# The second branch's gate columns moved to the front of an encoder layer, as two groups of 2x2 block quads

## The chip, the cores and the metric

The kernel runs on one core of one Trainium2 chip. The metric is device time in microseconds; the kernel before has a median of 1356.09 us over three runs (1355.71 to 1360.79). The names in the profile: PE is TensorE (matmuls; PEld its weight loads), DVE VectorE, ACT ScalarE, POOL GpSimd, and SP the engine that issues most transfers.

## The reference

One layer of an encoder over 256 tokens of width 2048, all in fp32. What matters here is the token-mixing half:

```python
h = rms_norm(x, g_mix)
proj = h @ w_in          # columns: c_q 512, c_kv 512, k_r 64, q_d, k_d, v_d 1024 each, gate 2 x 2048
c_q, c_kv, k_r, q_d, k_d, v_d, gate = jnp.split(proj, cuts, axis=-1)
...
y_a = o_a.reshape(B, S, MLA_HEADS * V_DIM) @ w_o_mla     # o_a: latent attention
y_b = o_b.reshape(B, S, dh) @ w_o_dil                    # o_b: dilated attention
g = jax.nn.sigmoid(gate + b_gate).reshape(B, S, 2, D_MODEL)
x = x + (g[:, :, 0] * y_a + g[:, :, 1] * y_b) @ w_o
gt, up = jnp.split(rms_norm(x, g_ffn) @ w_gate_up, 2, axis=-1)
return x + (jax.nn.silu(gt) * up) @ w_down
```

The gates depend on x and w_in alone, so they may be computed at any point before y_a and y_b are merged. The first branch's gates are gate columns 0 to 2047, the second's 2048 to 4095.

## The kernel before

**Products.** Every fp32 operand is split into a high part (a cast by ACT) and a low part (the rest, a subtraction by DVE), and each product is three matmuls: high by high, high by low, low by high (`mm3`, lines 428 to 431). The split itself is `split_pair` (lines 221 to 223), used for weights, which stream once through the chip, and for activations. x is transposed on PE in pairs of 128-column blocks k (`job_x`); `split_evac` (lines 205 to 219) takes a transposed pair out of PSUM, scaled by `g_mix`, as high part xTh (ACT, L214) and low part xTl (DVE, L219).

**Groups.** The work is a list of groups, each some columns of one weight matrix by all of its rows k. A group's weights come in chunks of 512 KB: SP loads a chunk into one of three buffers `x` (pool `xp`), ACT and DVE split it into one of six buffers of pool `wp`, and PE multiplies. `loads` and `splits` run a fixed number of chunks ahead of the products (`AHEAD`). In a group of w_in a chunk is two k, split as a 128x1024 cast and a 128x1024 subtraction. The list was: cq, ckv, group b0 of the dilated q, k, v, then four times (uq, ukv, b), b5, b6, the first branch's four gate groups `g0`, then for each j an output group of the latent attention, a gate group of the second branch, and an output group of the dilated attention (one behind), then four groups of w_o, and the FFN.

**Quads.** The FFN's w_gate_up groups are wider: gate and up columns together, 1024, and one step, a quad, is a 2x2 arrangement of blocks (two k, two column halves), multiplied into eight PSUM banks that are held for the whole stage. A plain quad has 8 block products, 24 matmuls. Quads 2, 4 and 6 (`FAST`) are multiplied with 7 block products, 21 matmuls, from sums of blocks: on the weights' side `split_fast` (lines 843 to 855) makes three additions on DVE and two further splits (rh/rl and r) before the wh/wl split; on the activations' side `job_h` (lines 615 to 635) copies the transposed blocks out as hs, and makes sums of them and splits them into hsh and hsl. `evac_fast` and `evac_pair` combine the banks at the end of the fast products and of the group.

**Order.** Up to the last two groups ahead of the FFN the program stands in written order (`in_order`, a manual schedule); after that a scheduler orders each engine's instructions by priority. Small jobs (transpositions, statistics of x, pieces of the attentions) are queued in `jobs` and `limited`, and one advances after each step; `needs` finishes a job at once when a product depends on it. Gate values went: banks, one `scalar_tensor_tensor` per token half (scale by 1/rms, add bias, L571), sigmoid on ACT (`evac_ya` for the first branch at its use, `evac_g1` at once for the second), and stayed in SBUF tiles until `evac_ya` and `evac_yb`. Each bias row is loaded by SP, broadcast over 128 partitions, 8 steps ahead.

Of the kernel before, what the change touches and what calls it, by code (L numbers as in the profile page):

```python
# [97 lines left out]
def layer_kernel(ctx: ExitStack, tc: tile.TileContext, a: dict, out: bass.AP):  # L98
# [142 lines left out]
    def transpose_in(act, k0, nk, src, gname=None):  # L241
# [315 lines left out]


# [15 lines left out]
    def evac_g0(j):  # L574
        def evac(ps, step):
            g0[j] = gate_evac(ps, j, f"g0_{j}")
        return evac

    def evac_ya(j):
# [3 lines left out]
        return evac  # L583
# [31 lines left out]
    def job_h(i):  # L615

        ps = half_side(f"tr_h{i}").rearrange("p (k s) -> p k s", s=S)
        for k in range(2):
            f = 2 * i + k
            for t in range(NT):  # L620
                nc.tensor.transpose(ps[:, k, t * P:(t + 1) * P], x1[f // 4][:, t, (f % 4) * P:(f % 4 + 1) * P], ident)
        g = [gain("g_ffn", 2 * i + k) for k in range(2)]
        if i not in EITHER:
            hP[i] = t4([P, 2, 2, S], f"hP{i}", F32R)
            split_evac(*((hP[i][:, 0, k], hP[i][:, 1, k], ps[:, k], g[k]) for k in range(2)))
        else:
            v, l, h = (t4([P, 8, P], f"{n}{i}", d) for n, d in (("hs", F32), ("hsl", F32R), ("hsh", F32R)))
            nc.scalar.activation(v[:, 0:8:7], ps[:, 0].rearrange("p (t s) -> p t s", t=NT), AF.Copy, scale=g[0])
            nc.scalar.activation(v[:, 1:3], ps[:, 1].rearrange("p (t s) -> p t s", t=NT), AF.Copy, scale=g[1])
            nc.vector.tensor_sub(v[:, 3], v[:, 7], v[:, 2])  # L630
            nc.vector.tensor_sub(v[:, 4], v[:, 7], v[:, 0])
            nc.vector.tensor_sub(v[:, 5], v[:, 0], v[:, 3])
            nc.vector.tensor_sub(v[:, 6], v[:, 1], v[:, 5])
            split_pair(h, l, v)
            hq[i] = (h, l)
        return
        yield
# [22 lines left out]
    def evac_fast(q):  # L660

        bank, z, u = held["q"], t4([P, NT, 512], f"z{q.group.c0}"), t4([P, NT, 512], f"u{q.group.c0}")
        add, sub = nc.vector.tensor_add, nc.vector.tensor_sub
        with tc.high_priority(offset=PRIO):
            nc.scalar.copy(u[:, 0], bank[1])
            sub(z[:, 0], bank[6], u[:, 0])
            add(u[:, 1], bank[7], z[:, 0])
            add(z[:, 1], bank[5], u[:, 1])
            add(z[:, 0], bank[5], z[:, 0])
        q.group.zu = z, u  # L670

    def evac_pair(half, i, last):

        def evac(zu, step):
            q = held["q"]
            z, u = zu
            add, sub = nc.vector.tensor_add, nc.vector.tensor_sub
            with tc.high_priority(offset=PRIO):
                add(z[:, 1], q[0], z[:, 1])
                add(z[:, 0], q[3], z[:, 0])  # L680
                add(u[:, 0], q[2], u[:, 0])
                sub(u[:, 1], q[4], u[:, 1])
# [44 lines left out]
    g_in(0, 512, evac_lat("cq"), sizes=[1, 1])  # L727
# [8 lines left out]
    for j in range(4):  # L736
        g_in(OFF_GATE + 512 * j, 512, evac_g0(j))
# [335 lines left out]
```

## Time and profile before

| | |
|---|---|
| median of three runs | 1356.09 us (1355.71 to 1360.79) |
| profiled execution | 1359.88 us, span 1358.1 us |
| mean granted clock of TensorE | 0.998 |
| matmuls on PE | 6243 |
| HBM read, written | 253.97 MB, 2.10 MB |

The page says how busy each engine was; the table of waits says, for each line of an engine, what its instructions waited for, how long in total, how often, and the longest. A row of a timeline gives the start in us, the duration, the engine, the line, the operation, the output and inputs by the program's names, the shapes, and in brackets the idle time before it and its releaser. A row of groups gives busy us in total, mean ns of one, and the idle time before the group's instructions with what ended it.

### The profile page before, as it was taken

Reading aid. Unit: us, or ns where it says so; the run is one execution under the profiler, and the core shown is the slowest. Engines: PE = TensorE matmul, PEld = TensorE weight load, DVE = VectorE, ACT = ScalarE, POOL = GpSimd, SP = SyncE. Lnnn points to the kernel's source line nnn. Section 1 sums busy time; section 2 is a strip of 40 time slices with the busy share of each in tenths; the row PEclk is TensorE's granted clock in tenths of the full one; section 3 lists DMA queues with packets and bytes.
Section 4 is the critical chain, followed back from the end, with each engine's and each line's share of the span. In section 5 each row is a group of like instructions: output and inputs, shape, how many; then the busy total and the mean of one; then the engine's idle time right before and its main releaser. Section 6 shows DMA issues by size and latency. Waiting matters only on the chain.

```text
span 1358.1 us, 16258 instructions
## 1 busy us (share of the span) xinstructions
PE 1338.5 (99%) x6243; PEld 1125.7 (83%) x6243; DVE 945.2 (70%) x916; ACT 653.0 (48%) x724; POOL 33.7 (2%) x41
## 2 busy tenths in 40 slices
PE   7999999999999999999999999999999999999998
PEld 5899999988888888888787888888878888888786
DVE  5567677677645555666789746886788579857973
ACT  6555655454444444455455433554445345434541
POOL 1010112000000000000000000000000000000000
PEclk9999999999999999999999999999999999999999
DMA  7555555656556665676545655556457555654662
GB/s 235 189 175 153 162 167 170 185 161 176 170 189 205 213 187 201 209 226 205 201 166 193 224 190 174 212 197 205 156 186 238 196 186 174 227 188 163 211 214 93
DMA packets 138733, 257.14 MB, mean 189 GB/s; under 512 B 9720, under 2 KB 29216, under 8 KB 138656
## 3 DMA queue, kind: packets, MB, share of 16 engines
q1 hardware_dynamic: 138288, 255.96, 58.1%
q8 instruction: 49, 0.80, 0.2%
q14 instruction: 28, 0.23, 0.1%
q10 hardware_dynamic: 144, 0.13, 0.0%
q0 software_dynamic: 224, 0.01, 0.0%
HBM read 253.97 MB, written 2.10 MB: 189 GB/s over the span
## 4 chain that ended last, share of the span: by engine, by line
PE 86%; DVE 5%; DMA 4%; issue 2%; ACT 2%; SPq 1%; DVEq 0%; ACTq 0%
PE g L431 14%; PE g L429 14%; PE g L430 14%; PE sC L429 5%; PE sC L430 5%; PE sC L431 5%; PE mA L429 3%; PE mA L431 3%; PE mA L430 3%; DMA x<-in_w_gate_up_dram 3%; PE sD L430 3%; PE sD L429 3%; PE sD L431 3%; PE mB L431 2%; PE mB L430 2%
## 5 line engine op out<-in xcount | busy, mean ns | idle before, releaser
L222 ACT CAST wh<-x 128x1024 fp32r<-128x1024 f32 (+3 forms) x349 | 465.0, 1352 | 427.9 <-DVE x L854 94.8
L223 DVE TENSOR_TENSOR wl<-x,wh 128x2048 fp32r<-128x2048 f32 x132 | 300.8, 2289 | 136.7 <-ACT wh L222 135.3
L223 DVE TENSOR_TENSOR wh<-x,wh 128x1024 fp32r<-128x1024 f32 (+2 forms) x217 | 250.7, 1172 | 110.2 <-ACT wh L222 108.7
L429 PE MATMUL g<-wh,xTh 128*128 128x512 f32 (+1 forms) x544 | 210.5, 387 | 2.1 <-ACT xTh L214 2.1
L431 PE MATMUL g<-wh,xTl 128*128 128x512 f32 (+1 forms) x544 | 207.9, 382 | 0.5 <-DVE xTl L219 0.5
L430 PE MATMUL g<-wh,xTh 128*128 128x512 f32 (+1 forms) x544 | 207.9, 382 | 0.0
L429 PEld LDWEIGHTS g<-wh,xTh 128*128 128x128 f32 x544 | 102.8, 189 | 17.5 <-ACT xTh L214 2.4
L431 PEld LDWEIGHTS g<-wh,xTl 128*128 128x128 f32 x544 | 102.9, 189 | 17.3 <-DVE xTl L219 1.0
L430 PEld LDWEIGHTS g<-wh,xTh 128*128 128x128 f32 x544 | 102.8, 189 | 15.4 <-DVE wh L223 0.3
L429 PE MATMUL sC<-wh,hP 128*128 128x512 f32 x220 | 86.1, 391 | 4.1 <-ACT z L685 2.3
L429 PE MATMUL sD<-wh,hP 128*128 128x512 f32 x220 | 85.7, 389 | 0.0
L431 PE MATMUL sD<-wh,hP 128*128 128x512 f32 x220 | 85.7, 389 | 0.0
L431 PE MATMUL sC<-wh,hP 128*128 128x512 f32 x220 | 85.6, 389 | 0.0
L430 PE MATMUL sC<-wl,hP 128*128 128x512 f32 x220 | 85.6, 389 | 0.0
L430 PE MATMUL sD<-wl,hP 128*128 128x512 f32 x220 | 85.6, 389 | 0.0
L222 ACT CAST rh<-x 128x1024 fp32r<-128x1024 f32 x33 | 34.7, 1051 | 44.6 <-DMA x<-in_w_gate_up_dram 44.6
L429 PEld LDWEIGHTS sC<-wh,hP 128*128 128x128 f32 x220 | 41.3, 188 | 14.9 <-issue 6.5
L429 PE MATMUL g<-wh,mTh 128*128 128x512 f32 x128 | 50.5, 394 | 0.0
L431 PE MATMUL g<-wh,mTl 128*128 128x512 f32 x128 | 49.9, 390 | 0.0
L430 PE MATMUL g<-wh,mTh 128*128 128x512 f32 x128 | 49.8, 389 | 0.0
L430 PEld LDWEIGHTS sD<-wl,hP 128*128 128x128 f32 x220 | 41.3, 188 | 8.7
L429 PEld LDWEIGHTS sD<-wh,hP 128*128 128x128 f32 x220 | 41.3, 188 | 8.7
(674 smaller groups left out, 2383.0 us busy)
## 6 DMA issues: line engine op xcount, KB each, us to landing
x<-in_w_gate_up_dram SPq DMA_DIRECT2D x143, 512.0 KB, 5.0
x<-in_w_down_dram SPq DMA_DIRECT2D x88, 512.0 KB, 5.1
x<-in_w_in_dram SPq DMA_DIRECT2D x79, 512.0 KB, 3.7
x<-in_w_in_dram SPq DMA_DIRECT2D x56, 448.0 KB, 3.5
x<-in_w_gate_up_dram SPq DMA_DIRECT2D x66, 256.0 KB, 3.0
x<-in_w_o_dram SPq DMA_DIRECT2D x32, 512.0 KB, 4.5
x<-in_w_o_mla_dram SPq DMA_DIRECT2D x16, 512.0 KB, 4.9
x<-in_w_o_dil_dram SPq DMA_DIRECT2D x16, 512.0 KB, 4.7
```

The lines of the kernel that those rows point to most:

```text
L222: nc.scalar.copy(h, x)
L223: nc.vector.tensor_sub(l, x, f32(h))
L429: nc.tensor.matmul(ps, ah, bh, start=first, stop=False)
L430: nc.tensor.matmul(ps, ah, bl, start=False, stop=False)
L431: nc.tensor.matmul(ps, al, bh, start=False, stop=last)
```

## The change

The first group is now the first branch's gate group 0 (with the small first chunks that cq had), then follow the second branch's gates as two quad groups of 1024 columns (gate columns 0 and 1, then 2 and 3, of 512 each), with the first branch's gate group 1 between them; then cq, ckv and the rest in their old order, with gate groups 2 and 3 of the first branch where all four were. In the quad groups quads 2, 4 and 6 are fast (`FAST_X`); for these, unsplit copies of x's transposed blocks are made when x is transposed (`copy_blocks`), and sums and splits of them a little later (`sums_of`, which the FFN now uses too, with 7 blocks split instead of 8). The finished second-branch gates (after sigmoid) and the unsigmoided values of the first branch's groups 0 and 1 are written to DRAM by GpSimd, 6 writes of 512 KB, and read back by SP 8 steps before their use. Bias rows are loaded by GpSimd. The manual order is left for the groups 1 to 3 and entered again after them. Ahead of the FFN the jobs that transpose the second half of its input get a high priority. Matmuls: 6225 for 6243. Table loads on ACT (`ACT_TABLE_LOAD`): 7 for 3.

```diff
+FAST_X = (2, 4, 6)
+    def copy_blocks(v, ps, g):
+        nc.scalar.activation(v[:, 0:8:7], ps[:, 0].rearrange("p (t s) -> p t s", t=NT), AF.Copy, scale=g[0])
+        nc.scalar.activation(v[:, 1:3], ps[:, 1].rearrange("p (t s) -> p t s", t=NT), AF.Copy, scale=g[1])
+    def sums_of(v, name):
+        h, l = t4([P, 7, P], f"hsh{name}", F32R), t4([P, 7, P], f"hsl{name}", F32R)
+        nc.vector.tensor_sub(v[:, 3], v[:, 7], v[:, 2])
+        nc.vector.tensor_sub(v[:, 4], v[:, 7], v[:, 0])
+        nc.vector.tensor_sub(v[:, 5], v[:, 0], v[:, 3])
+        nc.vector.tensor_sub(v[:, 6], v[:, 1], v[:, 5])
+        split_pair(h, l, v[:, :7])
+        return h, l
...
     def job_x(k0, nk):
-        transpose_in(xT, k0, nk, ...)
+        ps = transpose_in(xT, k0, nk, ...)
+        if nk == 2 and k0 // 2 in FAST_X:
+            xv[k0 // 2] = v = t4([P, 8, P], f"xv{k0}")
+            copy_blocks(v, ps, [gain("g_mix", k0 + k) for k in range(2)])
...
+    def job_xq(i):
+        xq[i] = sums_of(xv.pop(i), f"x{i}")
...
     def load_bias(c):
-        nc.sync.dma_start(b, ...)
+        nc.gpsimd.dma_start(b, ...)
...
     def evac_g0(j):
         def evac(ps, step):
+            xstat.finish(step)
             g0[j] = gate_evac(ps, j, f"g0_{j}")
+            if j < 2:
+                nc.gpsimd.dma_start(gd[j], g0[j])
+    def load_gate(j, to, k):
+        to[k] = t4([P, NT, 512], f"gd{j}")
+        nc.sync.dma_start(to[k], gd[j])
+    def evac_gates(j):
+        def evac(zu, step):
+            combine(zu)
+            for e in range(2):
+                for t in range(NT):
+                    nc.vector.scalar_tensor_tensor(zu[e][:, t], zu[e][:, t], st["x"][:, t:t + 1], gbias[4 + j + e],
+                                                   op0=ALU.mult, op1=ALU.add)
+                nc.scalar.activation(zu[e], zu[e], AF.Sigmoid)
+                nc.gpsimd.dma_start(gd[2 + j + e], zu[e])
...
-    def evac_g1(j):
-        def evac(ps, step):
-            tj[j] = gate_evac(ps, 4 + j, f"g1_{j}")
-            nc.scalar.activation(tj[j], tj[j], AF.Sigmoid)
...
     def job_h(i):
+        with tc.high_priority(offset=PRIO if i >= 4 else 0):
             ...
-    g_in(0, 512, evac_lat("cq"), sizes=[1, 1])
+    g_in(OFF_GATE + 512 * 0, 512, evac_g0(0), sizes=[1, 1])
+    for j in (0, 2):
+        groups.append(Group(W["w_in"], OFF_GATE + 2048 + 512 * j, 1024, range(NPAIR), xT, evac_gates(j),
+                            {k: (lambda k=k: [xqjob[k]]) for k in FAST_X}, fast=FAST_X))
+        if not j:
+            g_in(OFF_GATE + 512 * 1, 512, evac_g0(1))
+    g_in(0, 512, evac_lat("cq"))
...
-    for j in range(4):
+    for j in range(2, 4):
         g_in(OFF_GATE + 512 * j, 512, evac_g0(j))
...
     for j in range(4):
         out_mla(j)
-        g_in(OFF_GATE + 2048 + 512 * j, 512, evac_g1(j))
-        if j:
-            out_dil(j - 1)
-    out_dil(3)
+    for j in range(4):
+        out_dil(j)
...
+    jobs.extend(xqjob.values())
+    for j in xqjob.values():
+        j.ready = 9
...
-        if first and gi == ffn_at - 2:
+        if first and gi in (1, ffn_at - 2):
             in_order.close()
+        if first and gi == 4:
+            in_order.enter_context(tc.manual_schedule())
...
-        if gi == ffn_at and not held:
+        if q and not held:
             hold_banks()
+        elif held and 3 < gi < ffn_at:
+            held.clear()
+            spare.clear()
```

How this moves the engines' instructions is seen at three places. Names carry a buffer number behind the last underscore.

**The end of the first group.** ACT's rows before, from the transposition of x's blocks 12 and 13 on:

```order
L214 ACTIVATE xTh_301<-tr_xT_296,gmix 128x256 x2
L222 CAST wh_307<-x_253 128x1024
L273 ACTIVATE sqx_324,ssx<-xn_91 128x512 x2
L214 ACTIVATE xTh_301<-tr_xT_327,gmix 128x256 x2
L222 CAST wh_336<-x_282 128x1024
```

And now, with the semaphores that a row waits for; x_261 holds quad 0's weights, x_324 the first fast quad's, x_291 quad 1's:

```order
L213 ACTIVATE xTh_311<-tr_xT_306,gmix 128x256 [waits PE_49]
L213 ACTIVATE xTh_311<-tr_xT_306,gmix 128x256
L256 ACTIVATE xv_317<-tr_xT_306,gmix 128x2x128 [waits DVE_49]
L257 ACTIVATE xv_317<-tr_xT_306,gmix 128x256
L221 CAST wh_320<-x_261 128x2048 [waits DMAHW4_49,DMAHW3_49,Activation_49]
L301 ACTIVATE sqx_340,ssx<-xn_91 128x512 [waits DMAHW5_49]
L301 ACTIVATE sqx_340,ssx<-xn_91 128x512
L213 ACTIVATE xTh_311<-tr_xT_343,gmix 128x256 [waits PE_49]
L213 ACTIVATE xTh_311<-tr_xT_343,gmix 128x256
L221 CAST rh_352<-x_324 128x1024 [waits DMAHW1_49]
```

Two copies of x's blocks (xv) now stand between xTh of blocks 12 and 13 and the next cast; the first of them waits for DVE; the cast behind them is quad 0's, 2048 wide; and behind the last xTh the fast quad's casts (rh) come ahead of quad 1's.

**The first two quads.** On DVE, from the low part of quad 0's weights on:

```order
L222 TENSOR_TENSOR wl_321<-x_261,wh_320 128x2048
L218 SCALAR_TENSOR_TENSOR xTl_312<-tr_xT_343,gmix,xTh_311 128x256 x2
L222 TENSOR_TENSOR rl_353<-x_324,rh_352 128x1024
L222 TENSOR_TENSOR r_354<-x_324,r_354 128x512
L899 TENSOR_TENSOR x_324<-x_324 128x1024
L900 TENSOR_TENSOR x_324<-x_324 128x512
L901 TENSOR_TENSOR x_324<-x_324 128x512
L222 TENSOR_TENSOR wl_363<-x_291,wh_362 128x2048
L222 TENSOR_TENSOR wl_382<-x_324,wh_381 128x2048
L304 TENSOR_REDUCE ssx_404<-ssx 128x2
L622 SCALAR_TENSOR_TENSOR g_0_410<-g_147,rx,bias_130 128x512 x2
L183 TENSOR_TENSOR gcol<-gcol 128x1
```

On PE, in quad 0, where bank sD's products go on with quad 1's weights (wh_362, wl_363):

```order
L457 MATMUL sD<-wh_320,xTh_115 128x512
L458 MATMUL sD<-wl_321,xTh_115 128x512
L459 MATMUL sD<-wh_320,xTl_116 128x512
L457 MATMUL sD<-wh_362,xTh_115 128x512 [waits Activation_49]
L458 MATMUL sD<-wl_363,xTh_115 128x512 [waits DVE_49]
L459 MATMUL sD<-wh_362,xTl_116 128x512
L457 MATMUL sD<-wh_362,xTh_115 128x512
L458 MATMUL sD<-wl_363,xTh_115 128x512
L459 MATMUL sD<-wh_362,xTl_116 128x512
L457 MATMUL sC<-wh_320,xTh_115 128x512 [waits Activation_49]
L458 MATMUL sC<-wl_321,xTh_115 128x512
```

PE asks for quad 1's low weights after half of quad 0; DVE has five instructions of the fast quad, on x_324, ahead of them (rl, r, three sums; its last split, wl_382, stands behind). The first group's evacuation (L622) stands behind that.

**Two later places on ACT.** Now, around the first exponential of the latent attention (mla0p) (before, the same rows without the table load):

```order
L221 CAST wh_1903<-x_1851 128x2x384
L221 CAST wh_1949<-x_1883 128x1024
L364 ACTIVATE qd_1646<-g_1766,rx 128x448
L364 ACTIVATE qd_1647<-g_1766,rx 128x448
L536 ACT_TABLE_LOAD
L536 ACTIVATE mla0p,mla0mx<-mla0s,mla0mx 128x256 x4
L221 CAST wh_1972<-x_1906 128x1024
```

A table load stands directly ahead of the exponential; before, it stood ahead of the first sigmoid, far behind. And ahead of the FFN, at its last transposed pairs (hs, in bank mA), before:

```order
L222 CAST wh_5154<-x_5082 128x2048
L222 CAST wh_5209<-x_5112 128x2048
L628 ACTIVATE hs_5189<-mA,gcol 128x2x128
L629 ACTIVATE hs_5189<-mA,gcol 128x256
L222 CAST hsh_5191<-hs_5189 128x1024
```

And now:

```order
L221 CAST rh_5215<-x_5183 128x1024
L221 CAST r_5217<-x_5183 128x512
L256 ACTIVATE hs_5260<-mA,gcol 128x2x128
L257 ACTIVATE hs_5260<-mA,gcol 128x256
L221 CAST wh_5225<-x_5153 128x2048
L221 CAST hsh_5263<-hs_5260 128x896
```

The copies into hs (L628 and L629, now L256 and L257) stood behind the casts of two quads and now stand ahead of the next quad's cast, wh_5225.

More of the change, by code (lines that the diff above doesn't have):

```diff
@@ L97, in layer_kernel @@
 @with_exitstack
-def layer_kernel(ctx: ExitStack, tc: tile.TileContext, a: dict, out: bass.AP):
+def layer_kernel(ctx: ExitStack, tc: tile.TileContext, a: dict, out: bass.AP, gd: bass.AP):
     nc = tc.nc
@@ L556, in layer_kernel, with evac_fast, combine @@
         attn["dil", p] = Job(job_attn("dil", p), [prep["qd"], prep["kd"], bdone["vd"]])
+    def evac_fast(q):
+        bank, z, u = held["q"], t4([P, NT, 512], f"z{q.group.c0}"), t4([P, NT, 512], f"u{q.group.c0}")
+        add, sub = nc.vector.tensor_add, nc.vector.tensor_sub
+        with tc.high_priority(offset=PRIO):
+            nc.scalar.copy(u[:, 0], bank[1])
+            sub(z[:, 0], bank[6], u[:, 0])
+            add(u[:, 1], bank[7], z[:, 0])
+            add(z[:, 1], bank[5], u[:, 1])
+            add(z[:, 0], bank[5], z[:, 0])
+        q.group.zu = z, u
+    def combine(zu):
+        q = held["q"]
+        z, u = zu
+        add, sub = nc.vector.tensor_add, nc.vector.tensor_sub
+        with tc.high_priority(offset=PRIO):
+            add(z[:, 1], q[0], z[:, 1])
+            add(z[:, 0], q[3], z[:, 0])
+            add(u[:, 0], q[2], u[:, 0])
+            sub(u[:, 1], q[4], u[:, 1])
     g0, tj, mT, gbias = {}, {}, Act("mT", KD), {}
@@ L615, in job_h @@
     def job_h(i):
[L617 to L635, printed above, removed]
+        with tc.high_priority(offset=PRIO if i >= 4 else 0):
+            ps = half_side(f"tr_h{i}").rearrange("p (k s) -> p k s", s=S)
+            for k in range(2):
+                f = 2 * i + k
+                for t in range(NT):
+                    nc.tensor.transpose(ps[:, k, t * P:(t + 1) * P], x1[f // 4][:, t, (f % 4) * P:(f % 4 + 1) * P], ident)
+            g = [gain("g_ffn", 2 * i + k) for k in range(2)]
+            if i not in FAST:
+                hP[i] = t4([P, 2, 2, S], f"hP{i}", F32R)
+                split_evac(*((hP[i][:, 0, k], hP[i][:, 1, k], ps[:, k], g[k]) for k in range(2)))
+            else:
+                v = t4([P, 8, P], f"hs{i}")
+                copy_blocks(v, ps, g)
+                hq[i] = sums_of(v, str(i))
         return
@@ L658, in layer_kernel @@
     sg, hidT, djobs = {}, {}, {}
[L660 to L670, printed above, removed]
     def evac_pair(half, i, last):
         def evac(zu, step):
-            q = held["q"]
             z, u = zu
[L677 to L682, printed above, removed]
+            combine(zu)
             r = st["2"]
@@ L761, in layer_kernel @@
             needs = {k: (lambda k=k: [hjobs[k]]) for k in range(NPAIR)}
-            fast = FAST_1 if half and not i else FAST
-            needs[2] = lambda: list(hjobs.values())
+            needs[FAST[0]] = lambda: list(hjobs.values())
             if i:
-                needs[2] = lambda half=half, i=i: [djobs[half, i - 1]]
-            groups.append(Group(W["w_gate_up"], 512 * j, 1024, range(NPAIR), None, evac_pair(half, i, i == len(js) - 1), needs, None, fast))
+                needs[FAST[0]] = lambda half=half, i=i: [djobs[half, i - 1]]
+            groups.append(Group(W["w_gate_up"], 512 * j, 1024, range(NPAIR), None, evac_pair(half, i, i == len(js) - 1), needs))
         for j in range(4):
@@ L884, in products_quad @@
             h, l = w
-            def factors(kk, t):
-                if q.i in EITHER:
-                    return (z[:, BLOCK[kk, t]] for z in hq[q.i])
-                return (hP[q.i][:, e, kk, t * P:(t + 1) * P] for e in range(2))
             for t, n in ((1, 0), (0, 0), (0, 1), (1, 1)):
@@ L912, in products @@
         final = gi == len(groups) - 1
-        if first and gi < ffn_at:
+        if first and gi < ffn_at and not held:
             ps = psm.tile([P, NT, 512], F32, name=f"g{gi}", tag="main")
@@ L916, in products @@
         elif first:
-            ps = held[DOWN[g.c0 // 512]]
+            ps = held["A" if gi < ffn_at else DOWN[g.c0 // 512]]
             gps[gi] = [ps, ps[:, 0], ps[:, 1]]
```

50 lines of the change are left out of this document (33 added, 17 removed).

## The prediction

> **What bounds the kernel now.** The page's head and the table of PE's waits come first:
>
> ```profile
> span 1358.1 us, 16258 instructions
> PE 1338.5 (99%) x6243; PEld 1125.7 (83%) x6243; DVE 945.2 (70%) x916; ACT 653.0 (48%) x724; POOL 33.7 (2%) x41
> ...
> GB/s 235 189 175 153 162 167 170 185 161 176 170 189 205 213 187 201 209 226 205 201 166 193 224 190 174 212 197 205 156 186 238 196 186 174 227 188 163 211 214 93
> ...
> q1 hardware_dynamic: 138288, 255.96, 58.1%
> ```
>
> ```profile
> engine line waited for: us in total, times, longest us
> PE mA L621 <- ACT hs L629: 2.5, 1, 2.5
> PE sC L429 <- ACT z L685: 2.3, 2, 1.2
> PE g L429 <- ACT xTh L214: 2.1, 1, 2.1
> PE sC L429 <- DVE u L681: 1.7, 3, 1.1
> PE sD L693 <- DVE z L687: 0.7, 2, 0.6
> ```
>
> TensorE is busy for 99% of the span, so the time is the number of its matmuls plus what it waits, some tens of microseconds in all. A change pays by taking matmuls away or by removing a wait, and costs by each stall that it makes; the other engines' busy time matters only where it makes PE wait. All matmuls of the weight groups have one shape, and their spacing is the unit of this sum. The timeline of PE shows two of them:
>
> ```profile
> 38.67 0.39 PE L431 MATMUL g<-wh,xTl 128*128 128x512 f32 x1
> 57.05 0.39 PE L431 MATMUL g<-wh,xTl 128*128 128x512 f32 x1
> ```
>
> Between them lie 81 intervals: 18.38 / 81 = 0.227 us from start to start (the 0.39 is a duration that overlaps its neighbours).
>
> **A: fewer matmuls, −4.1.** The second branch's gates were four groups of 96 matmuls. They become two groups of eight quads, five plain ones of 24 matmuls and three fast ones of 21, 183 each for 192. So 18 go, 18 × 0.227 = 4.1 us. That is all the change can take from PE's work. The average quad takes PE (5 × 24 + 3 × 21) / 8 × 0.227 = 5.2 us. By the groups of DVE instructions of one shape,
>
> ```profile
> L223 DVE TENSOR_TENSOR wl<-x,wh 128x2048 fp32r<-128x2048 f32 x132 | 300.8, 2289 | 136.7 <-ACT wh L222 135.3 <-PE g L431 0.8
> L852 DVE TENSOR_TENSOR x<-x 128x1024 f32<-128x1024 f32 x33 | 40.3, 1221 | 0.6
> L223 DVE TENSOR_TENSOR rl<-x,rh 128x1024 fp32r<-128x1024 f32 x33 | 40.2, 1219 | 10.7 <-ACT rh L222 10.6
> L853 DVE TENSOR_TENSOR x<-x 128x512 f32<-128x512 f32 x33 | 22.7, 689 | 0.8
> L223 DVE TENSOR_TENSOR r<-x,r 128x512 fp32r<-128x512 f32 x33 | 22.6, 684 | 2.1 <-ACT r L222 2.1
> ```
>
> a plain quad's weights cost DVE 2.29, a fast one's 1.22 + 0.68 + 1.22 + 2 × 0.69 + 2.29 = 6.8 (L854 does as L853 does), on average (5 × 2.29 + 3 × 6.8) / 8 = 4.0 a quad. DVE keeps up in the mean, but a fast quad alone is slower to prepare (6.8) than to multiply (4.8), and these stand where nothing has been prepared ahead.
>
> **H: the wait ahead of the FFN, −2.0 (0 to −2.5).** The largest wait of the table is one place:
>
> ```profile
> 649.37 0.39 PE L431 MATMUL sC<-rh,hsl 128*128 128x512 f32 x1
> 652.26 0.66 PE L621 MATMUL mA<-ident,x 128*128 128x128 f32 x4 [2.50 <-ACT hs L629]
> ```
>
> ```profile
> 649.57 1.90 ACT L222 CAST wh<-x 128x2048 fp32r<-128x2048 f32 x1 [4.48 <-issue]
> 651.74 0.47 ACT L629 ACTIVATE hs<-mA,gcol 128x256 f32<-128x256 f32 x1
> ```
>
> The last transposition needs the bank that the copies into hs empty, and these stand behind a cast that itself had to wait for a buffer. In the new order the copies stand ahead of the next quad's cast, and the two transpositions are 17 matmuls apart, not 9. The copies are then free of the 1.90 and have 8 × 0.227 = 1.8 us more, together above 2.5; I take 2.0, as the cast now behind them is late by their 0.8.
>
> **Bias, +0.9 (0.7 to 1.1).** The first group is now a gate group, so its bias (128 copies of 2 KB, 256 KB) is loaded at the start, by POOL. The DMA is full there, by windows (length; busy PE, PEld, DVE, ACT, POOL with counts; PEclk; DMA share; GB/s):
>
> ```profile
> 9.10:12.30 3.20, 2.63 (x14) 1.82 (x14) 0.92 (x1) 1.05 (x1) 0.00 (x0) 1.00 1.06 386
> 12.30:15.70 3.40, 1.25 (x4) 0.77 (x5) 2.49 (x5) 3.03 (x5) 0.00 (x0) 1.00 0.84 267
> 15.70:19.10 3.40, 3.40 (x9) 2.52 (x9) 3.07 (x4) 2.82 (x7) 0.00 (x0) 0.51 0.98 324
> ```
>
> 256 KB at 386 GB/s are 0.7 us, at the 235 of the page's first slice (its row of GB/s) 1.1; all later loads shift by that, and PE waits for loads here.
>
> **Clock, +0.9 (0 to 3.4).** The same rows show a window in which PE was busy 1.25 of 3.40, and the next at a granted clock of 0.51, which loses half of 3.4, 1.7 us. The stalls below fall within 40 us of there. I take half a chance of one more such window, and two as the upper end.
> The Trainium skill (TensorE: Matmul & The Clock Gate, "Part 1: The HAM clock gate") halves the clock after at least one idle window of about 3.4 us. By that the stalls below, each under 3 us, would throttle nothing, and the sum would be 0.9 lower; the rows above show a throttled window behind one that was a third busy, which the rule read strictly does not give.
>
> **B: the end of the first group, +1.4 (0 to 2.8).** Its fast quads need unsplit copies of x's blocks 4, 5, 8, 9, 12 and 13, six ACT copies more, as large as hs above (0.47). Before:
>
> ```profile
> 30.10 1.05 ACT L222 CAST wh<-x 128x1024 fp32r<-128x1024 f32 x1
> 31.04 0.64 ACT L273 ACTIVATE sqx<-xn 128x512 f32<-128x512 f32 x1
> 32.56 0.84 ACT L214 ACTIVATE xTh<-tr_xT,gmix 128x256 fp32r<-128x256 f32 x2 [0.18 <-PE tr_xT L246]
> ```
>
> ```profile
> 30.24 0.88 DVE L219 SCALAR_TENSOR_TENSOR xTl<-tr_xT,gmix,xTh 128x256 fp32r<-128x256 f32 x2 [1.03 <-ACT xTh L214]
> ```
>
> ```profile
> 35.12 0.39 PE L429 MATMUL g<-wh,xTh 128*128 128x512 f32 x1
> ```
>
> The last matmul is the first of k = 14. In the new order the copies of blocks 12 and 13 stand between xTh(12, 13) and the next cast, and the first of them waits for DVE's xTl pair. On the old clock: pair done 31.1 (30.24 + 0.88), 0.2 later for the earlier copies; two copies, 32.1; the cast is now that of a quad, 1.9 (as at 649.57), 34.0; two squares, 35.3; the first xTh 35.7. PE wants it at 35.12: 0.6 to 0.8 late. DVE's wl behind the cast takes 34.0 + 2.3 = 36.3, xTl(14) 36.8, and PE's third matmul, at 35.57 + 0.7, waits another 0.6. Sum 1.4. The upper end is all that ACT and DVE have more in this piece: 2 × 0.42 + (1.91 − 1.05) + (2.29 − 1.22) = 2.8. At the lower end the transfers, not this chain, set the end.
>
> **C: the first quads' weights, +2.6 (0 to 3.6).** PE's order takes quad 1's products on bank sD after only 12 products of quad 0. DVE has five of the first fast quad's instructions (4.5) ahead of quad 1's wl (2.29): 6.8 less their overlaps, about 6.3, from the end of xTl(14, 15) at 37.4: 43.7. PE leaves the first group at 37.84 + 1.4, and with the small transposition of the gains (0.3), 12 × 0.227 and the first product of quad 1 it asks for wl at 42.2: 1.5 late. If the fast quad's third transfer lands late too, more:
>
> ```profile
> ACT rh L222 <- DMA x<-in_w_gate_up_dram: 44.6, 25, 3.6
> ```
>
> In the FFN ACT waits for a fast quad's load in 25 of 33 cases, 44.6 / 25 = 1.8 us each, though there loads run far ahead. With 1.8 on top it is 3.3, and with overlaps unfavourable 3.6. The middle is 2.6: the DMA is near full until here, so a late load is about as likely as not.
>
> **D: the first low factors of x, +0.5 (0 to 2).**
>
> ```profile
> L571 DVE SCALAR_TENSOR_TENSOR g<-g,rx,bias 128x512 f32<-128x512 f32 x16 | 11.3, 744 | 17.2 <-PE g L431 17.2
> L223 DVE TENSOR_TENSOR wh<-x,wh 128x896 fp32r<-128x896 f32 x56 | 60.1, 1086 | 9.2 <-ACT wh L222 8.7
> 46.91 0.19 POOL L201 TENSOR_SCALAR rx_v<-ssx 128x2 f32<-128x2 f32 x1 [41.75 <-DVE ssx L276]
> 47.18 0.72 POOL L203 TENSOR_TENSOR rx<-rx_v,mhalf 128x2 f32<-128x2 f32 x1
> ```
>
> The low halves of x's seven blocks (1.09, as the 128x896 split) stand on DVE behind wl of quad 2 (2.29, done 46.0), the first group's evacuation (0.9 for POOL's two steps, then 2 × 0.74), wl of quad 3 (2.29) and the next fast quad's first two (1.22 + 0.68): done at 53.7 to 54.4. PE reaches them at 39.2 + 0.3 + 1.5 + 55 × 0.227 (two quads and 7 matmuls) = 53.5, or 53.9 with its other small work, so 0 to 0.5. I take 0.5; if POOL is late, held by the writes that are issued on its queue, up to 2.
>
> **F: starts of the two quad groups, +0.9 (0 to 1.5).** The FFN's 11 quad groups wait 2.3 + 1.7 + 0.7 at their starts for the evacuation of the last group (second table), 0.43 each; 2 × 0.43.
>
> **E: table loads, +1.1 (0 to 1.3).**
>
> ```profile
> 376.20 1.28 ACT L581 ACT_TABLE_LOAD   x1
> 120.34 1.23 DVE L512 TENSOR_TENSOR mla0p<-mla0p,mla0mx 128x1024 f32<-128x1024 f32 x1
> 121.77 1.03 PE L519 MATMUL mla0pt<-ident,mla0p 128*128 128x128 f32 x8
> 278.23 1.22 DVE L512 TENSOR_TENSOR dil0p<-dil0p,dil0mx 128x1024 f32<-128x1024 f32 x1
> 282.30 1.03 PE L519 MATMUL dil0pt<-ident,dil0p 128*128 128x128 f32 x8
> ```
>
> With sigmoids before the attentions, ACT's table goes sigmoid, exp, sigmoid, exp, sigmoid, silu: four loads more. Only the one ahead of the first exp of mla0 stands on a tight chain: DVE's result is ready at 121.57, PE takes it at 121.77, a slack of 0.2. 1.28 − 0.2 = 1.1. The first dilated one has 282.30 − 279.45 = 2.9 of slack.
> The Trainium skill (ScalarE: Activation LUTs, "Table sets: the hidden batching unit") says to do all work of one set before switching, which this order does not, and gives about 2.7 us a switch; by that E would be 2.5 and the sum 1.4 higher. The row says 1.28.
>
> **At nothing.** Gate values: 6 writes and 6 reads of 512 KB, 2.5% of the queue's 256 MB, beside a DMA that is 58% busy; if the cover goes, one late reload is about 1.5 us at 386 GB/s. The gates' STTs and sigmoids move with their groups and stay off PE's path but for D and F. The FFN's fast factors fall from 8 blocks to 7, off the path. POOL's small rstd work queues behind issues of writes only, with whole groups in between.
>
> **Sum.** −4.1 − 2.0 + 0.9 + 0.9 + 1.4 + 2.6 + 0.5 + 0.9 + 1.1 = +2.2, against the profiled execution's 1359.9 us (span 1358.1, and 1.8 around it): 1362.1. That execution lies 3.8 above the median of the runs, 1356.1, near the top of their spread; the difference carries over, so I predict **1358.3**. All terms at their favourable ends give −4.1 − 2.5 + 0.7 = −5.9, 1350.2; all at the others +11.6, 1367.7.
>
> **Rivals.**
> R1, the gain stays: the first groups wait for transfers, not for DVE or ACT, so B to F hide behind waits that are there anyway. −4.1 − 2.0 + 0.7 = −5.4, 1350.7. For it: DMA at 0.84 to 1.06 until 19 us. Against it: from 38.67 to 57.05 PE ran without a gap while quads now have to be prepared.
> R2, slower: the early fast quads get no lead. Each of the six waits the 1.8 us that ACT waits for such a load in the FFN, and here PE feels it: 6 × 1.8 = 10.7 in place of C, D and F (4.0). +2.2 − 4.0 + 10.7 = +8.9, 1365.0. It decides once the first fast quad's last load lands after 37.7, when DVE would take it up. For it: three buffers for loads, and no group ahead that loads slower than it computes. Against it: in the FFN these waits did not reach PE.
> R3, the change doesn't shorten PE's stream: what the fast quads save is waited for elsewhere, A is gone, +6.3, 1362.4. Against it: DVE's 4.0 a quad under PE's 5.2.
>
> **How the numbers follow.** My forecast 0.58, R1 0.15, R2 0.20, R3 0.07. The range is 1351.0 to 1367.0: it leaves out the last piece of R1 and of the upper ends. What this kernel's measurement can tell from no change is about 0.5%, 6.8 us: under 1349.3 is faster, over 1362.9 slower. Faster: 0.4 of R1 and a trace of the forecast, 0.07. Slower: 0.06 of the forecast's 0.58, 0.17 of R2, half of R3, 0.27. Within: 0.66.
>
> **What would show it.** A: 6225 matmuls, and a spacing of 0.227 still. H: no wait of 2.5 at the last transposition. B, C, D: PE waits for xTh and xTl near 36, for a wl near 43 and for the low factors near 54, of 1.4, 2.6 and 0.5. E: a wait for mla0p near 250 (121.8 and the 558 matmuls put ahead), behind ACT_TABLE_LOAD. Clock: one more slice under 1.0 before 60. If PE's waits up to 140 us sum to over 12, R2 holds; if under 1, R1. The forecast is wrong if loads of w_in arrive late throughout, or if gate writes on POOL hold up rx.

## The result and the profile after

The changed kernel has a median of 1363.14 us (1360.29 to 1370.54, 19 runs), the one before 1358.81 us (1355.14 to 1364.16, 19 runs) beside it. The ratio is 1.0038, 95% interval 1.0027 to 1.0048: slower by about 5 us, clear of the scatter but under the half per cent that was called no change. The profiled execution has a span of 1362.2 us, 4.1 over the one before. The page of the changed kernel, its head and the queue that the gate writes and bias rows now use (packets, MB, share of the 16 engines):

```profile
span 1362.2 us, 16319 instructions
...
PE 1336.1 (98%) x6225; PEld 1120.7 (82%) x6225; DVE 984.3 (72%) x961; ACT 670.7 (49%) x735; POOL 42.2 (3%) x55
...
q0 software_dynamic: 1728, 5.26, 1.3%
```

The 18 matmuls are gone and PE is less busy by 2.4 us, but the span is longer: the difference lies in time that PE does not work, mostly waits. The waits of PE in the changed kernel from 20 to 245 us, where the kernel before had none:

```profile
PE sD L458 <- DVE wl L222: 2.2, 2, 1.8
PE mA L458 <- DVE wl L222: 1.7, 1, 1.7
PE g L457 <- ACT xTh L213: 1.0, 1, 1.0
PE mA L459 <- DVE hslx L222: 0.9, 1, 0.9
PE g L459 <- DVE xTl L218: 0.4, 1, 0.4
```

Where they stand, in PE's timeline, with three more rows that the text below uses:

```profile
7.54 0.66 PE L245 MATMUL tr_xT<-ident,xn 128*128 128x128 f32 x2 [3.48 <-DMA xn<-in_x_dram]
...
15.31 0.50 PE L457 MATMUL g<-wh,xTh 128*128 128x512 f32 x1 [2.16 <-ACT xTh L213]
...
37.03 0.50 PE L457 MATMUL g<-wh,xTh 128*128 128x512 f32 x1 [0.96 <-ACT xTh L213]
38.16 0.50 PE L459 MATMUL g<-wh,xTl 128*128 128x512 f32 x1 [0.39 <-DVE xTl L218]
45.90 0.50 PE L458 MATMUL sD<-wl,xTh 128*128 128x512 f32 x1 [1.84 <-DVE wl L222]
56.96 0.50 PE L459 MATMUL mA<-r,hslx 128*128 128x512 f32 x1 [0.88 <-DVE hslx L222]
...
122.50 0.50 PE L458 MATMUL mA<-wl,hshx 128*128 128x512 f32 x1 [1.72 <-DVE wl L222]
...
259.61 1.06 PE L547 MATMUL mla0pt<-ident,mla0p 128*128 128x128 f32 x8 [1.21 <-DVE mla0p L540]
...
646.49 0.66 PE L686 MATMUL mA<-ident,x 128*128 128x128 f32 x4 [1.22 <-DVE x L701]
```

Points of equal work in the two timelines give the stages. The first products of k = 2 and the last transposition ahead of w_o, before:

```profile
13.90 0.50 PE L429 MATMUL g<-wh,xTh 128*128 128x512 f32 x1 [2.12 <-ACT xTh L214]
...
550.85 1.03 PE L246 MATMUL tr_mT<-ident,g 128*128 128x128 f32 x8
```

and of the changed kernel the second of these:

```profile
558.20 1.03 PE L245 MATMUL tr_mT<-ident,gd 128*128 128x128 f32 x8
```

Up to there the changed kernel has lost 558.20 − 550.85 = 7.35 us although its 4.1 us of matmuls are already saved, so 11.4 us were lost: 2.7 by the end of the first group, 6.9 in the three gate groups behind it, 1.6 up to mla0pt, 0.2 after. From there on it gains 3.2 us: 1.2 at the FFN's start and 2.0 behind it, where the waits of PE for the FFN's evacuations (u and z) fell from 4.7 us in all to 3.3.

A wait costs about 0.3 us more than the idle time in its bracket; this is called its restart below. From start to start, the wait of 1.84 takes 2.56 us from the product ahead of it (43.68) to the one behind it (46.24), where two steps of 0.227 are 0.45: 2.1 us lost.

### The profile page after: what moved, and what is told of

It is laid out like the page before. It is cut to its first block, busy times and chain, and to the rows that moved or that the text cites. A ratio compares the mean times of both kernels' runs of the same rounds, so it can differ in the third digit from the quotient of the medians.

```text
span 1362.2 us, 16319 instructions
## 1 busy us (share of the span) xinstructions
PE 1336.1 (98%) x6225; PEld 1120.7 (82%) x6225; DVE 984.3 (72%) x961; ACT 670.7 (49%) x735; POOL 42.2 (3%) x55
## 4 chain that ended last, share of the span: by engine, by line
PE 81%; DVE 4%; issue 2%; DMA 2%; ACT 2%; SPq 0%; DVEq 0%; ACTq 0%
PE g L457 10%; PE g L458 10%; PE g L459 10%; PE sC L457 6%; PE sC L458 5%; PE sC L459 5%; PE mA L458 4%; PE mA L457 4%; PE mA L459 4%; PE sD L459 4%; PE sD L457 4%; PE sD L458 4%; PE mB L457 3%; PE mB L459 3%; PE mB L458 2%
## 5 line engine op out<-in xcount | busy, mean ns | idle before, releaser
L221 ACT CAST wh<-x 128x2048 fp32r<-128x2048 f32 (+3 forms) x333 | 462.9, 1408 | 432.8 <-DVE x L901 98.3
L222 DVE TENSOR_TENSOR wl<-x,wh 128x2048 fp32r<-128x2048 f32 x148 | 336.9, 2288 | 150.5 <-ACT wh L221 147.3
L222 DVE TENSOR_TENSOR wh<-x,wh 128x1024 fp32r<-128x1024 f32 (+3 forms) x185 | 212.6, 1163 | 78.2 <-ACT wh L221 77.2
L457 PE MATMUL g<-wh,xTh 128*128 128x448 f32 (+1 forms) x384 | 147.6, 384 | 3.1 <-ACT xTh L213 3.1
L459 PE MATMUL g<-wh,xTl 128*128 128x448 f32 (+1 forms) x384 | 145.4, 379 | 1.2 <-DVE xTl L218 0.9
L458 PE MATMUL g<-wh,xTh 128*128 128x448 f32 (+1 forms) x384 | 144.9, 377 | 0.0
L459 PEld LDWEIGHTS g<-wh,xTl 128*128 128x128 f32 x384 | 72.4, 189 | 12.9 <-DVE xTl L218 2.9
L457 PEld LDWEIGHTS g<-wh,xTh 128*128 128x128 f32 x384 | 72.5, 189 | 12.8 <-ACT xTh L213 3.8
L458 PEld LDWEIGHTS g<-wh,xTh 128*128 128x128 f32 x384 | 72.5, 189 | 9.0
L221 ACT CAST rh<-x 128x1024 fp32r<-128x1024 f32 x39 | 41.0, 1052 | 65.6 <-DMA x<-in_w_gate_up_dram 52.7
L222 DVE TENSOR_TENSOR rl<-x,rh 128x1024 fp32r<-128x1024 f32 x39 | 47.6, 1219 | 17.8 <-ACT rh L221 17.8
```

The source lines that it names most:

```text
L221: nc.scalar.copy(h, x)
L222: nc.vector.tensor_sub(l, x, f32(h))
L457: nc.tensor.matmul(ps, ah, bh, start=first, stop=False)
L458: nc.tensor.matmul(ps, ah, bl, start=False, stop=False)
L459: nc.tensor.matmul(ps, al, bh, start=False, stop=last)
```

## The experiments

Ratios are to the kernel before, each over the runs of its own batch; the changed kernel's 1.0038 stands beside them.

**Bias rows behind the first group's loads.**

```diff
-        nc.gpsimd.dma_start(b, ...)
+        (nc.sync if c in (0, 4) else nc.gpsimd).dma_start(b, ...)
...
-        at(gidx("evac_g0", j), lambda j=j: load_bias(j), 0 if j < 2 else 8)
+        at(gidx("evac_g0", j), lambda j=j: load_bias(j), (-5, 0, 8, 8)[j])
```

> Edit: the bias rows of the first group and of the first column of the first quad group are issued on SP's queue behind the first group's loads, not by POOL at the program's start; the rest as changed. My theory (the early broadcast of 2 x 256 KB takes transfer time from x and the first weights): PE's wait for the second transposition falls from 3.48 to about 1.0 us, the first matmul of k = 2 starts some 1.4 us earlier, and the whole is 1.0 to 1.5 us under the changed kernel, ratio to before about 1.003. Rival (the lead is lost again at the end of the first group, where ACT and DVE set the pace): the wait falls but the wait for xTh at k = 14 grows by as much, ratio 1.004 as the changed kernel.

Ratio 1.0035, 1.0016 to 1.0053. The timeline of PE in this kernel:

```profile
5.01 0.66 PE L245 MATMUL tr_xT<-ident,xn 128*128 128x128 f32 x2 [0.94 <-DMA xn<-in_x_dram]
...
13.70 0.50 PE L457 MATMUL g<-wh,xTh 128*128 128x512 f32 x1 [1.82 <-ACT xTh L213]
...
36.24 0.51 PE L459 MATMUL g<-wh,xTl 128*128 128x512 f32 x1 [0.39 <-DVE xTl L218]
```

The wait went from 3.48 to 0.94, k = 2 came 1.6 us earlier, and at the first group's end 1.9 us were still in hand (36.24 against 38.16): my theory, in the trace. In the time an effect of 0.001 is within the interval, so the runs do not decide between the two expectations. The profiled execution lost the lead again to the clock (and the twelve executions had a mean granted clock of 0.9983, the changed kernel's 19 one of 0.9992). Its windows (columns as in the prediction):

```profile
40.80:44.20 3.40, 1.42 (x8) 0.84 (x6) 3.37 (x4) 2.12 (x2) 0.00 (x0) 1.00 0.01 2
44.20:47.60 3.40, 3.40 (x8) 2.73 (x9) 2.28 (x3) 1.08 (x5) 0.91 (x2) 0.50 0.70 201
```

**Sigmoids after the reload.**

```diff
     def evac_gates(j): ...
-                nc.scalar.activation(zu[e], zu[e], AF.Sigmoid)
     def evac_yb(j): ...
+            nc.scalar.activation(tj[j], tj[j], AF.Sigmoid)
             nc.vector.tensor_mul(tj[j], ps, tj[j])
```

> Edit: the second branch's gates go to DRAM without their sigmoid, which is applied after the reload, when the dilated output is merged. My theory (the table load ahead of the first exponential is the wait): PE's wait for mla0p, 1.21 us, is gone, with its restart 1.4 us, two table loads fewer, ratio to before about 1.0028. Rival (DVE or ACT is late there for the order of the jobs, not for the table): a wait of about 1 us stays, ratio 1.004.

Ratio 1.0021, 1.0007 to 1.0035. PE no longer waits there; the row carries no bracket:

```profile
257.41 1.03 PE L547 MATMUL mla0pt<-ident,mla0p 128*128 128x128 f32 x8
```

The table load was the wait: in the five other runs that keep the early sigmoids, and with them this load, PE waits 1.2 us there each time. The ratio fell by 0.0017, 2.3 us, a little more than the 1.4 us and within its interval.

**Plain quads only in the early groups.** 18 matmuls more than the changed kernel.

```diff
-FAST_X = (2, 4, 6)
+FAST_X = ()
...
-            combine(zu)
+            zu = [t4([P, NT, 512], f"{n}g{j}") for n in "zu"]
...
-   nc.vector.scalar_tensor_tensor(zu[e][:, t], zu[e][:, t], ...)
+   nc.vector.scalar_tensor_tensor(zu[e][:, t], held["q"][PLAIN[t, e]], ...)
```

> Edit: the two early quad groups have no fast quads: 18 matmuls more, no copies of x's blocks, no sums; the gates are scaled straight out of their banks. My theory (DVE's preparation of the early fast quads has no lead): the waits for wl near 46, 109 and 122 us and for hslx near 57 go, 5.5 to 6 us with their restarts, and about 0.8 at the end of the first group; against 4.1 us of matmuls the whole is 2 to 3 us under the changed kernel, ratio about 1.002. Rival (the weights land late whoever prepares them): the waits stay behind the casts, and the ratio is 1.0038 + 4.1/1358 = 1.007.

Ratio 1.0010, 0.9995 to 1.0024. Between 20 and 245 us the table of PE's waits is empty: all of the waits at the first group's end, for wl and for hslx are gone. The kernel is faster by some 3.8 us (0.0028) than the changed one, with 4.1 us of matmuls more. So the early fast quads, with all that belongs to them, cost about 8 us and save 4. The traces agree: from the first product of k = 2 to mla0pt the changed kernel takes 244.3 us and this one 238.5, that is 9.9 us lost against 4.1 saved.

**Other quads fast: 3, 5, 6.**

```diff
-FAST_X = (2, 4, 6)
+FAST_X = (3, 5, 6)
```

> Edit: the fast quads of the two early groups are 3, 5 and 6 instead of 2, 4 and 6; as many matmuls as changed. My theory (what is late is the order on DVE, where the first fast quad stands ahead of quad 1's low weights): the wait for wl near 46 goes (2.1 us with its restart), that for hslx goes or halves (0.7 to 1.3), a wait of up to 1 us may come where quads 5 and 6 follow each other, ratio about 1.002. Rival (a lack of DVE time, which only moves with the fast quads): the same 5 to 6 us of waits in other places, ratio 1.004.

Ratio 1.0053, 1.0035 to 1.0071: my theory's 1.002 is out, the rival's 1.004 is not; against the changed kernel's 1.0038 the intervals overlap. All waits from 20 to 245 us come to 9.1 us, over the changed kernel's 6.2. Those for wl near 46 us and for hslx near 57 went, as expected (1.0 us behind ACT stayed near 46), but PE's timeline has new ones where quads 5 and 6 follow each other, in both groups:

```profile
69.69 0.50 PE L457 MATMUL mA<-wh,hshx 128*128 128x512 f32 x1 [1.06 <-ACT wh L221]
72.65 0.51 PE L458 MATMUL mA<-wl,hshx 128*128 128x512 f32 x1 [2.00 <-DVE wl L222]
...
142.86 0.50 PE L457 MATMUL mA<-wh,hshx 128*128 128x512 f32 x1 [0.56 <-ACT wh L221]
145.18 0.50 PE L458 MATMUL mA<-wl,hshx 128*128 128x512 f32 x1 [1.82 <-DVE wl L222]
```

Two fast quads in a row ask 13.6 us of DVE (2 × 6.8) against 9.5 of PE. So it isn't only the order of the first fast quad on DVE: the waits moved to where two fast quads follow each other, as a lack of DVE's time would make them.

**Gate writes of the first quad group 70 us later.**

```diff
-                nc.gpsimd.dma_start(gd[2 + j + e], zu[e])
+                late.append((gd[2 + j + e], zu[e]))
+            if j:
+                for dst, src in late:
+                    nc.gpsimd.dma_start(dst, src)
```

> Edit: the two 512 KB writes of the first quad group's gates are issued together with those of the second, 70 us later; the rest as changed. My theory for the two waits at the start of the second quad group (wl near 109 us, 0.35, and near 122 us, 1.72): the loads there share the transfer engines with these writes and two bias rows (window 100 to 104 us, DMA share 1.03), so the weights land late; without the writes both waits together fall under 0.7 us and the whole by 1 to 2 us, ratio about 1.003. Rival (DVE's order: the first group's leftovers, L622 and the fast quad's sums, stand ahead of wl): the waits stay between 1 and 2 us in sum and the ratio at 1.004.

Ratio 1.0025, 1.0011 to 1.0039. The small wait near 109 us is under the 0.15 us from which a wait is listed; the large one stays:

```profile
121.44 0.50 PE L458 MATMUL mA<-wl,hshx 128*128 128x512 f32 x1 [1.77 <-DVE wl L222]
```

So the 1.7 us do not belong to the writes. That the 0.35 us do is not shown: the kernels with late bias rows and with late sigmoids leave the writes as they are, and lack that wait too. The timelines of ACT and of DVE in the changed kernel show what stands ahead of the large one:

```profile
117.26 1.05 ACT L221 CAST rh<-x 128x1024 fp32r<-128x1024 f32 x1 [6.08 <-DMA x<-in_w_in_dram]
118.21 1.90 ACT L221 CAST wh<-x 128x2048 fp32r<-128x2048 f32 x1
```

```profile
116.23 0.68 DVE L901 TENSOR_TENSOR x<-x 128x512 f32<-128x512 f32 x1
118.34 1.22 DVE L222 TENSOR_TENSOR rl<-x,rh 128x1024 fp32r<-128x1024 f32 x1 [1.44 <-ACT rh L221]
120.15 2.29 DVE L222 TENSOR_TENSOR wl<-x,wh 128x2048 fp32r<-128x2048 f32 x1 [0.58 <-ACT wh L221]
```

The first fast quad's sums are done at 116.9, but its cast wh stands on ACT behind rh of the next fast quad, which waits for its load until 117.26; on DVE the next quad's rl stands ahead of wl in turn. So an order again, together with a load. No run changed this order alone, but in the two kernels just named, with the same order, the load comes earlier against PE and the wait is 0.6 and 1.0 us instead of 1.7.

**The written order kept through the quad groups.**

```diff
-        if first and gi in (1, ffn_at - 2):
+        if first and gi == ffn_at - 2:
             in_order.close()
-        if first and gi == 4:
-            in_order.enter_context(tc.manual_schedule())
```

> Edit: the manual order is kept through the two quad groups, so no scheduler reorders them; the rest as changed. My theory (the scheduler's order on DVE and PE makes the wait at 46 us): with the written order PE takes quad 0 whole before quad 1, so wl of quad 1 has 12 matmuls, 2.7 us, more, and the wait of 1.84 goes; but the evacuations and the splits are no longer interleaved, and waits of 1 to 3 us come at the first fast quad. Sum of PE's waits in 40 to 190 us 3 to 5 us, ratio 1.003 to 1.005. Rival (DVE's time alone): the same 4.8 us of waits in other places.

Ratio 1.0181, 1.0159 to 1.0202: both expectations missed, by some 19 us. PE's waits from 20 to 245 us:

```profile
PE sD L458 <- DVE wl L222: 8.6, 3, 3.9
PE sC L457 <- ACT gcol L182: 4.8, 1, 4.8
PE mA L457 <- ACT hshx L221: 2.6, 1, 2.6
```

and the windows around one of them:

```profile
122.40:125.80 3.40, 0.51 (x2) 0.41 (x3) 3.40 (x3) 1.90 (x1) 0.00 (x0) 0.96 0.00 0
125.80:129.20 3.40, 3.40 (x10) 2.69 (x9) 2.96 (x3) 0.00 (x0) 0.15 (x1) 0.54 0.80 252
```

There are four such places, each wait followed by a stretch at half the clock. All of PE's waits there come to 17.7 us, where the changed kernel has 6.2. These 11.5 us more, and five windows at half the clock (the first place has two), make up the 19. The reordering, which I had blamed for the wait at 46 us, is worth far more than that wait.

**The priority of the late transpositions alone, in the kernel before.**

```diff
+        with tc.high_priority(offset=PRIO if i >= 4 else 0):
+            ... (the body of job_h)
```

> Edit: the kernel before with one part of the change alone, the high priority of the jobs that transpose the second half of the FFN's input. My prediction's step H: the wait of 2.5 us at the last transposition goes, 2 us in sum, ratio 0.9985. Rival, after what the other kernels with this priority show (waits for x of 1.2 to 2.0 us at an earlier transposition): the wait moves to the residual addition, sum of PE's waits between 615 and 655 us 1.2 to 2.4 us, ratio 0.9995 to 1.0005.

Ratio 0.9992, 0.9977 to 1.0006, which holds both expectations. In the trace the wait moved, as the rival says:

```profile
616.80 1.09 PE L622 MATMUL tr_h<-ident,x 128*128 128x128 f32 x8 [1.73 <-DVE x L643]
640.75 0.66 PE L622 MATMUL mA<-ident,x 128*128 128x128 f32 x4 [1.07 <-DVE x L643]
```

The wait of 2.50 is gone, and the transpositions, now directly behind the residual addition, wait 2.8 us for it, more than the 2.4 that the rival allowed.

**Plain quads, late sigmoids and late bias rows together.** The edits of three kernels above, combined.

> Edit: the changed kernel with plain early quads, sigmoids after the reload, and the two early bias rows behind the first group's loads. If the single terms add up: plain quads alone gave 1.001; without the wait for mla0p (1.4 us) and without the early broadcast (1.6 to 1.9 us at the first group's end) the ratio is 0.9985 to 0.999, so nothing of the early gates costs time any more and nothing gains. Rival (what is taken away is given back later by waits in the FFN): ratio 1.001 as plain quads alone.

Ratio 0.9987, 0.9974 to 1.0001. The terms add up, and the rival's 1.001 is out. From 20 to 245 us PE waits for nothing that is listed.

**The same with quads 4 and 6 fast.**

```diff
-FAST_X = ()
+FAST_X = (4, 6)
```

The combining of the banks (`combine`), which plain quads do without, is back as well.

> Edit: as the kernel with plain early quads, late sigmoids and late bias rows, but quads 4 and 6 of the two early groups are fast: 12 matmuls fewer than with plain ones. My theory (a fast quad needs 6.8 us of DVE ahead of 4.8 us of PE, so it pays only behind plain quads, where DVE is ahead, and the copies for x's blocks 12 and 13 still delay the first group's end): no wait for wl or hslx over 0.5 us between 40 and 190 us, about 1.4 to 1.9 us at the end of the first group, so against plain quads -2.7 + 1.7 us, ratio to before 0.998 to 0.999. Rival (each fast quad next to another waits for its weights wherever it stands): 2 to 4 us of waits in the two groups, ratio 1.000 to 1.002.

Ratio 0.9961, 0.9945 to 0.9976 (six executions), faster than the kernel before and the changed one, and more than I expected: 0.998 to 0.999 lies outside. PE's waits from 20 to 245 us:

```profile
PE sD L458 <- DVE wl L222: 0.7, 1, 0.7
PE g L457 <- ACT xTh L213: 0.6, 1, 0.6
PE g L459 <- DVE xTl L218: 0.4, 1, 0.4
```

The end of the first group still costs 1.0 us of waits, with the copies for x's blocks 12 and 13, and one wait for wl is 0.7, not under 0.5. The large waits of the early fast quads are gone. But that fast quads gain anything here is not shown. The first product of k = 2 and the first transposition of mla0p, with plain quads and the two other edits:

```profile
13.21 0.50 PE L457 MATMUL g<-wh,xTh 128*128 128x512 f32 x1 [2.13 <-ACT xTh L213]
...
251.92 1.03 PE L547 MATMUL mla0pt<-ident,mla0p 128*128 128x128 f32 x8
```

and with quads 4 and 6 fast:

```profile
13.36 0.50 PE L457 MATMUL g<-wh,xTh 128*128 128x512 f32 x1 [2.04 <-ACT xTh L213]
...
250.33 1.03 PE L547 MATMUL mla0pt<-ident,mla0p 128*128 128x128 f32 x8
```

Between them lie 238.7 and 237.0 us. The first has a half-clock window at 15.5 us, about 1.4 us lost, and the second none; so of the 2.7 us of matmuls saved under half a microsecond is left. Behind mla0pt, where the two programs are edited alike, the second profile is 3.1 us shorter. The waits at the FFN's start and at its groups differ by that much from kernel to kernel, and no run isolates them, so most of the ratio's gain has no shown cause.

**The same with quads 3 and 5 fast.**

> Edit: the same with quads 3 and 5 fast, whose copies of x's blocks 6, 7, 10 and 11 come earlier in the first group. My theory: the wait at the first group's end shrinks under 0.5 us, as there are no copies behind the last transpositions but one; the waits of 3.1 us near 70 and 145 us that quads 5 and 6 together had go, one of about 1 us near 46 us (the gains' copy behind the fast quad's casts) stays: ratio 0.997 to 0.9985. Rival: the same waits near 70 and 145 us at quad 5, ratio 1.000 to 1.002.

Ratio 0.9973, 0.9961 to 0.9985. Nothing waits at the first group's end any more, and 0.3 us remains where quads 5 and 6 together had cost 3; the wait of 0.80 behind the gains' copy came as expected. In this trace too, k = 2 to mla0pt takes 238.5 us with a half-clock window at 15.5, so the 2.7 us saved are all but used up. By their intervals neither the two choices nor this one and plain quads can be told apart.

## Why the prediction was right or wrong

The range (1351 to 1367) held the time, and a difference within half a per cent, the likeliest case, is what came. The likeliest number was 1358.3 on the 1356.1 known then, +2.2 us; the ratio gives about +5.2 (3.7 to 6.5). The right sign of the sum is in part luck: B came out larger and the second quad group's waits, 2.6 us, had no term at all, while the clock and the FFN came out better than forecast. Term by term, forecast first, restarts counted:

- **A**, −4.1: as predicted, 6225 matmuls at the same spacing.
- **Bias**, +0.9: 1.4 us at k = 2 in this profile (15.31 against 13.90), 1.6 to 1.9 by the profile of the run that moved the loads. Single profiles scatter here: k = 2 begins at 13.8 to 15.3 us in the six with early rows and at 13.2 to 14.3 in the four changed kernels with late ones, 1.0 apart in the mean. I had counted one row of 256 KB; POOL issues the first at 1.47 us and the second at 7.31, behind a wait for the first, beside the loads of x.
- **Clock**, +0.9: −1.6 in these two profiles, the wrong sign. The half-clock window at 15.70:19.10 that I took from the profile before is not in the one after. The clock changes on a grid of 3.41 us (last section), and the waits near k = 2 fall into two windows of it, each over half busy:

```profile
10.90:14.30 3.40, 2.25 (x14) 1.71 (x12) 1.23 (x1) 1.08 (x2) 0.00 (x0) 1.00 0.99 345
14.30:17.70 3.40, 1.84 (x7) 1.22 (x8) 2.50 (x4) 2.89 (x6) 0.00 (x0) 1.00 1.00 333
```

  In the kernel before they fall into one. So the stalls that I added did not bring a window, and the one that was there went. Eight of the twelve profiles have at least one such window. Over the executions the mean granted clock is 0.9992 in the changed kernel (19) and 0.9986 in the kernel before (79, beside the other kernels).
- **B**, +1.4: the two listed waits, 0.96 and 0.39, are 1.9 with their restarts. With gaps too short to be listed, where the copies for x's earlier blocks stand, it is 2.9: from k = 2 to the end of the first group (its 96th product) the changed kernel takes 25.0 us and the one with plain quads, which has no copies, 22.1. The chain worked out was right for the last pair of blocks; for the earlier ones it had only 0.2.
- **C**, +2.6: idle 1.84, 2.1 lost. The DVE chain by itself (1.5) and the middle with a late load are about equally near: rh waited 0.7 us for its transfer.
- **D**, +0.5: idle 0.88, 1.1 lost.
- **E**, +1.1: idle 1.21, 1.4 lost. The load took 1.28 us, and 1.32 us lie between the end of the ACTIVATE ahead of it and the first exponential. The Trainium skill (ScalarE: Activation LUTs, "Table sets: the hidden batching unit") gives 2.7 for a switch; by that the wait would have been 2.5, as an estimate, and the trace does not agree.
- **F**, +0.9: the step failed. The two early groups do not wait at their starts for the evacuation. PE waits at the second group's first chunks and first fast quad instead, 0.35 + 1.72, 2.6 with restarts. The sum has no term for that: DVE's mean of 4.0 us a quad against PE's 5.2 was taken to cover what comes behind the first quads.
- **H**, −2.0: the step failed in size. −1.2 in this profile, and nothing measurable alone (0.9992): what is late next was the residual addition x, which I did not price.
- **At nothing**: the two gate writes that a run moved cost 0.35 us at the most; the other four and the reloads no run moved. Behind the FFN's start this profile is 2.0 us shorter, which no term had; the FFN's waits at group starts, between 0.15 and 1.3 us each, differ from kernel to kernel with the order, and no run isolates them.

Of the rivals, R2 had the right place but not the size: the first fast quad's load landed just after the 37.7 us from which it should decide (rh begins at 38.03 behind a wait), but only around the first fast quad of each group did PE lose more than a microsecond. Its sign was badly chosen: counted from the span's start PE's waits up to 140 us are 15.5, over the 12 that should show R2, but the kernel before has 7.4 of them too; from 20 us on, where it has none, they are 6.2, not 10.7. R1 is out: the waits for what DVE and ACT prepare are there, and plain quads take them away. R3 came nearest. PE's stream did become shorter, against its first words, but what the fast quads save was waited for elsewhere, and more than that (8 us lost, 4.1 saved); its +6.3 is nearer to the +5.2 than my +2.2, and what I held against it, DVE's mean under PE's, is the step that failed. I gave it 0.07.

## What to carry to other kernels

A trick that saves the busiest engine an eighth of a step and costs the next engine more than that step lasts can pay only where that engine is already ahead: not at the beginning of a stage, and not twice in a row. Behind steps that let it get ahead it paid back here what its preparation cost, and hardly more, as far as the traces show. When work is moved to the front of a program, price what goes with it: loads that an idle queue issues at once beside the first loads, and a function table that must be switched back. A wait removed by priority should be followed to what is late next before it enters the sum. A mean that fits (4.0 us against 5.2) says nothing of the first step, which has no lead.

## What the runs showed of the hardware

The half clock follows waits much shorter than 3.4 us (one of 1.98 in the run with late bias rows), and whether it does depends on where the wait falls. In every trace the granted clock changes only at multiples of 3.413 us from its first change; the kernel before loses it at 15.78 us and has it back at 19.20. So PE's busy time must be counted in windows of that grid. In the twelve profiles, from the first change at 8.5 to 13 us to the last matmuls, all eleven windows at the full clock with PE busy 1.45 us or less were followed by one at half (the run with late bias rows shows such a pair: 1.42, then 0.50). Of the windows with 1.66 or more, one was. The changed kernel's wait of 1.84 us at 46 us falls into two windows of its grid, and the clock stayed at 1.00:

```profile
41.60:45.00 3.40, 2.46 (x11) 1.69 (x9) 3.33 (x4) 1.19 (x1) 0.00 (x0) 1.00 0.11 41
45.00:48.40 3.40, 2.50 (x11) 1.97 (x12) 3.12 (x3) 2.01 (x6) 0.18 (x1) 1.00 0.43 130
48.40:51.80 3.40, 3.40 (x17) 2.79 (x16) 1.54 (x4) 1.87 (x2) 1.57 (x4) 1.00 0.96 327
```

The lowest window that kept the clock, in the run with late gate writes:

```profile
119.70:123.10 3.40, 1.66 (x7) 1.40 (x8) 3.40 (x3) 1.67 (x1) 0.00 (x0) 1.00 0.28 46
123.10:126.50 3.40, 3.40 (x16) 2.82 (x16) 3.33 (x4) 0.00 (x0) 0.00 (x0) 1.00 0.97 376
```

and the exception, with plain quads, late sigmoids and late bias rows:

```profile
12.10:15.50 3.40, 1.74 (x6) 1.16 (x7) 2.65 (x4) 3.14 (x6) 0.00 (x0) 1.00 1.01 324
15.50:19.00 3.50, 3.50 (x12) 2.79 (x11) 2.60 (x4) 2.35 (x6) 0.00 (x0) 0.51 0.96 303
```

In a half-clock window products start 0.427 us apart instead of 0.227, so it costs up to 3.41 × (1 − 0.227 / 0.427) = 1.6 us (an estimate from these spacings), about as much as the wait itself. This is part of the scatter of single executions: of 79 of the kernel before, the 19 with a granted clock of 1.000 have a median of 1356.6 us, the 18 with 0.997 or less one of 1361.7. So an effect of 1.5 us can show in a trace and not in a median of twelve.
